# Float32r parts for the weights-times-values products of an attention kernel, and three shared buffers for weight chunks and their low parts

## The chip, the cores and the metric

The kernel runs on one core of a Trainium2 chip. The metric is the device time of one execution in microseconds (us). A core has TensorE (PE, which also has a queue of weight loads, PEld), VectorE (DVE), ScalarE (ACT), GpSimd (POOL) and SyncE (SP, which here only issues DMAs). Each engine works through its own instructions in the order of its queue.

## The reference

Two blocks of two layers each run after one another on 512 tokens of 1024 features, in float32. What the change touches is the last step of every softmax attention: weights times values.

```python
# block 1, a layer: window attention and latent attention, 8 heads each, 512 tokens and 256 context tokens
p = jax.nn.softmax(jnp.concatenate([s_loc, s_ctx, s_sink], axis=-1), axis=-1)
o = (jnp.einsum('bnhgqk,bnkhd->bnqhgd', p_loc, vw) + jnp.einsum('bnhgql,blhd->bnqhgd', p_ctx, v_ctx))
...
p = jax.nn.softmax(s.astype(jnp.float32) * SCALE_B, axis=-1)
return jnp.einsum('bhqk,bkhd->bqhd', p.astype(vals.dtype), vals)
# block 2, a layer: two softmax mixers (6 heads each), a gated recurrence, then a gated feed-forward
return jnp.einsum('bhgqk,bhkd->bhgqd', p, vt)
...
return (jax.nn.silu(a) * b) @ w_down
```

All projections (in_proj, the branches' merge, w_o, w_up, w_down) are plain matrix products with weights from DRAM.

## The kernel before

Features lie on partitions, tokens along the free dimension. A projection `h @ w` is worked off in chunks of weights of 128 x 1024 values (512 KB). `wload` (L149 and on) fetches one: a DMA brings it into a buffer `wraw` (issued on SP, L162), ACT casts it to a float32r high part `wh` (`hi`, L139), and DVE subtracts that from the chunk, in two halves of 512 columns, to give the float32r low part `wl` (`lo`, L144). `mm3` (L174 and on, the product in L182) then multiplies by three of the four pairs of parts (high x high, high x low, low x high): 24 matmuls for each chunk and 512 tokens. `self.wb = (2, 2)` (in `block1`) gives two buffers to `wraw`, and two each to `wh` and `wl`. Chunks that are kept for later lie in tiles of another tag; of these only `wraw` comes from these buffers.

Block 1's first layer has 768 columns (tokens and context), its second layer 512. A layer goes through `attention` (scores, softmax, `pv_out`, with projections filled in between), `merge` (for each of 3 branches and 8 feature tiles a gate projection of one chunk, and a branch product of half a chunk: a branch chunk serves two feature tiles, so it is in use over half a product, a whole gate product and half a product), and `w_out`. Block 2's layers go through `mixers`, a `w_out_2` product in two halves of the tokens, and `ffn` (44 chunks of w_up, then 24 of w_down, of which every third is 384 KB). While `merge` and the first layer's `ffn` run, a generator `mod_steps` computes modulation vectors on DVE (L294) from further 512 KB loads (`mw`, L289).

`pv_out` (L527 and on) takes the normalised weights of two query tiles j = 0, 1 of one head. It transposes them on TensorE, 128 x 128 at a time and four to a group, into a PSUM tile `pt` (2 buffers), copies the group to SBUF in one ACT instruction (`pT`, 3 buffers), and multiplies each transposed tile by the values of its key block, in float32: values of 64 columns as the stationary operand, the two query tiles in the two halves of the array's columns, so of `pv`'s partitions. In the trace a float32 product is two matmul instructions. Two DVE copies (L547) take `pv` to `y`.

`schedule_with_timeline_sim=True`: the order of each queue, and which buffer of a tag a tile gets, are fixed when the kernel is built. SP's queue holds all loads and stores of the kernel, in one order.

Of the kernel before, what the change touches and what calls it, by code (L numbers as in the profile page):

```python
# [9 lines left out]
F32 = mybir.dt.float32  # L10
# [6 lines left out]
P = 128  # L17
# [13 lines left out]
class Cat:  # L31
    """Column ranges of one feature tile kept in two tiles, split at column 512."""
# [10 lines left out]
class Pools:  # L43
    """Two pools as one: the tags named lie in the second."""
# [8 lines left out]
class Halves:  # L53
    """A chunk of weights in two tiles of 512 columns."""
# [13 lines left out]
class Fill:  # L68
    """Steps of generators, emitted a few at a time among the steps of another stream."""
# [34 lines left out]
class Kern:  # L104
# [10 lines left out]
    def open(self):  # L115
# [5 lines left out]
        self.ones = self.cp.tile([P, P], F32, tag="ones", name="ones")  # L121
# [27 lines left out]
    def wload(self, src, kt, n, tag=None):  # L149
        """A chunk [128, kt*n] of weights as an exact sum of two float32r parts."""  # L150
# [23 lines left out]
    def mm3(self, ps, w, x, cols, n0=0, n1=P, ks=None, start=True, stop=True, o=0):  # L174
        """ps[n, t - o] += sum_k w[k][:, n] x[k][:, t] from split operands."""
# [9 lines left out]
    def seq(self, a, b):  # L185
        """Keeps b behind a in their engine's queue."""
# [3 lines left out]
    def after(self, ins):  # L190
        """Keeps ins behind the last product so far."""
# [3 lines left out]
    def rsqrt(self, v, n, inv, pool=True):  # L195
        """(v*inv + eps)^-0.5 of a small [128, n]: a first guess from the exponent, one step of third order, one of second."""
# [9 lines left out]
        # y * (15 - 10 a + 3 a^2) / 8  # L206
# [20 lines left out]
    def colsum(self, ps, a, nt):  # L227
        """ps[p, t] = sum over the partitions of a[:, t*128 + p]."""
# [3 lines left out]
    def rows(self, ps, r, nt):  # L232
        """ps[m, t*128 + p] = r[p, t] for every m."""
# [5 lines left out]
    def silu_cols(self, src, n, name, w):  # L239
        """[128, 8, w] with silu of n vectors in the first n columns, zeros elsewhere."""  # L240
        nc = self.nc
        c = self.kp.tile([P, KD, n], F32, tag=src, name=src)
        nc.sync.dma_start(c, self.A[src])
        t = self.kp.tile([P, KD, n], F32, tag=name + "_t", name=name + "_t")
        nc.scalar.activation(t, c, AF.Tanh, scale=0.5)
        s = self.kp.tile([P, KD, w], F32, tag=name, name=name)
        if w > n:
            nc.vector.memset(s, 0.0)
        u = self.kp.tile([P, KD, n], F32, tag=name + "_u", name=name + "_u")
# [4 lines left out]
    def mod_chunk(self, sc, n, wsrc, bias, layer, g, mt):  # L254
        """mt[:, 8g:8g+8, :] = 1024 outputs of s @ w + b for n vectors, on the tensor engine."""
# [10 lines left out]
        self.mod_rows(ps, n, bias, g, mt)  # L266

    def mod_rows(self, ps, n, bias, g, mt):
        """Output 256j + c of vector r, in row 32j + r and column c of ps, to features on partitions, plus bias."""
        nc = self.nc  # L270
        row = self.sm.tile([P, 256], F32, tag="modrow", name=self.nm("modrow"), bufs=1)
# [4 lines left out]
        # feature g*1024 + j*256 + s*128 + p sits in column s*128 + j*32 + r  # L276
# [6 lines left out]
    def mod_steps(self, sc, n, wsrc, bias, layer, g, mt):  # L283
        """The same with the products on the vector engine; one step a 128 rows of w."""
# [16 lines left out]
        self.mod_rows(ps, n, bias, g, mt)  # L301
# [37 lines left out]
    def norm_part(self, xs, mod, g, c0, c1, j, ishift, iscale, dst, tmp=None, acc=None, sq="t"):  # L339
        """Columns c0:c1 of h = rms_norm(x, g) * (1 + scale) + shift, split into the tiles that dst(k) gives; mod  # L340
# [1526 lines left out]
```

## Time and profile before

| | us |
|---|---|
| median of 3 runs | 3027.91 (3026.98 to 3037.3) |
| span of the profiled execution | 3026.6 |
| TensorE busy in it | 2920.6 |
| VectorE busy | 1924.7 |
| ScalarE busy | 1353.0 |

The profiled execution's span lies 1.3 us under the median of the runs; what lies around the span is within that, so a change of the span is taken as a change of the time. In the profile's rows a busy PE is not PE at its peak, since matmuls overlap: the spacing of their starts tells what one costs. The letters f32 and fp32r in a row's shapes are the operands' types; matmuls of float32r operands are printed as f32 too.

### The profile page before, as it was taken

To read this page: it belongs to the slowest core of one execution; us is meant where nothing else is said; L and a number is where in the kernel's file an instruction comes from. 1 tells how busy PE (TensorE), PEld (TensorE's weight loads), DVE (VectorE), ACT (ScalarE), POOL (GpSimd) and SP (SyncE) were. 2 spreads that over 40 slices of the span, in tenths; PEclk is the share of its full clock that TensorE was granted. 3 is DMA by queue.
4 is the path that set the end of the run, shared out by engine and by line. 5 is a ranking of instruction groups with operands and counts; after the bars stand their busy time and mean duration, and the time that the engine had idled before them with its cause. 6 is when DMAs were issued, how large, how long until landed. Compare 5 with 4: busy or idle time off the path is not lost.

```text
span 3026.6 us, 46233 instructions
## 1 busy us (share of the span) xinstructions
PE 2920.6 (96%) x17920; PEld 2417.4 (80%) x17920; DVE 1924.7 (64%) x3720; ACT 1353.0 (45%) x2414; POOL 261.5 (9%) x520
## 2 busy tenths in 40 slices
PE   7999999999998999999998998999999998999999
PEld 4888888888887888777778876788888876788887
DVE  5666555555556566656676777688853778576642
ACT  3445544322234345653225775544433675554421
POOL 2000000001112000000112212000000223000000
PEclk9999999999998999999999999999999999999999
DMA  6221111333342423124653211355543311233232
GB/s 236 76 69 53 55 63 64 116 127 124 119 160 85 126 80 106 52 69 174 232 201 132 76 47 48 105 177 200 189 142 115 97 43 53 85 100 97 98 107 89
DMA packets 113163, 331.76 MB, mean 110 GB/s; under 512 B 18160, under 2 KB 20720, under 8 KB 112944
## 3 DMA queue, kind: packets, MB, share of 16 engines
q1 hardware_dynamic: 112944, 328.81, 33.6%
q8 instruction: 141, 2.31, 0.3%
q14 instruction: 78, 0.64, 0.1%
HBM read 300.51 MB, written 17.76 MB: 105 GB/s over the span
## 4 chain that ended last, share of the span: by engine, by line
PE 84%; DVE 8%; ACT 2%; DMA 2%; issue 2%; POOL 2%; SPq 0%; DVEq 0%; ACTq 0%; POOLq 0%
PE mm L182 32%; PE up L182 15%; PE dn L182 11%; PE pu L182 5%; PE pv L544 4%; PE pt L539 4%; PE po L182 2%; PE s L851 2%; PE s L568 1%; PE s L1223 1%; DVE zz L1527 1%; DVE wl L144 1%; PE pre L182 1%; PE pq L182 1%; DMA yg<-yd 1%
## 5 line engine op out<-in xcount | busy, mean ns | idle before, releaser
L144 DVE TENSOR_TENSOR wl<-wraw,wh 128x512 fp32r<-128x512 f32 (+2 forms) x706 | 473.1, 709 | 391.3 <-ACT wh L139 382.8
L139 ACT CAST wh<-wraw 128x1024 fp32r<-128x1024 f32 (+4 forms) x364 | 365.8, 1005 | 754.2 <-PE mm L182 241.5
L182 PE MATMUL mm<-hh,wh 128*128 128x512 f32 (+1 forms) x1240 | 488.8, 397 | 9.2 <-ACT hh L373 3.5
L182 PE MATMUL mm<-hl,wh 128*128 128x512 f32 (+1 forms) x1240 | 487.9, 394 | 5.0 <-DVE hl L374 5.0
L182 PE MATMUL mm<-hh,wl 128*128 128x512 f32 (+1 forms) x1240 | 487.3, 393 | 0.0
L182 PEld LDWEIGHTS mm<-hh,wh 128*128 128x128 f32 x1240 | 235.0, 191 | 58.2 <-ACT wh L139 6.9
L182 PEld LDWEIGHTS mm<-hl,wh 128*128 128x128 f32 x1240 | 235.8, 190 | 50.3 <-DVE hl L374 7.0
L182 PEld LDWEIGHTS mm<-hh,wl 128*128 128x128 f32 x1240 | 235.5, 190 | 49.6 <-DVE wl L144 3.0
L182 PE MATMUL up<-hh,wh 128*128 128x512 f32 (+1 forms) x688 | 261.1, 381 | 3.8 <-DVE fu L1643 2.3
L182 PE MATMUL up<-hl,wh 128*128 128x512 f32 (+1 forms) x688 | 261.0, 380 | 0.5
L182 PE MATMUL up<-hh,wl 128*128 128x512 f32 (+1 forms) x688 | 261.2, 380 | 0.2 <-DVE wl L144 0.2
L541 ACT COPY pT<-pt 128x512 f32<-128x512 f32 (+1 forms) x304 | 159.5, 551 | 177.0 <-PE pt L539 175.7
L294 DVE SCALAR_TENSOR_TENSOR macc<-mw,sc,macc 128x1024 f32<-128x1024 f32 x140 | 181.0, 1308 | 74.1 <-DMA mw<-w_mod 38.8
L539 PE MATMUL pt<-ident,E 128*128 128x128 f32 x1120 | 174.7, 282 | 4.1 <-DVE E L551 3.4
L539 PEld LDWEIGHTS pt<-ident,E 128*128 128x128 f32 x1120 | 127.8, 142 | 39.6 <-issue 24.4
L182 PEld LDWEIGHTS up<-hh,wh 128*128 128x128 f32 x688 | 128.8, 188 | 30.2 <-ACT ah L139 2.7
L182 PEld LDWEIGHTS up<-hl,wh 128*128 128x128 f32 x688 | 129.1, 188 | 26.2 <-DVE hl L374 1.3
L182 PEld LDWEIGHTS up<-hh,wl 128*128 128x128 f32 x688 | 129.1, 188 | 25.8 <-DVE wl L144 0.9
L964 POOL TENSOR_TENSOR m<-m,gt 128x768 f32<-128x768 f32 (+1 forms) x32 | 54.5, 1704 | 1077.4 <-DVE gt L960 755.8
L182 PE MATMUL mm<-ch,wl 128*128 128x256 f32 x504 | 143.7, 285 | 0.0
L182 PE MATMUL mm<-cl,wh 128*128 128x256 f32 x504 | 143.2, 284 | 0.0
L182 PE MATMUL mm<-ch,wh 128*128 128x256 f32 x504 | 143.1, 284 | 0.0
(416 smaller groups left out, 6135.7 us busy)
## 6 DMA issues: line engine op xcount, KB each, us to landing
wraw<-w_in SPq DMA_DIRECT2D x158, 512.0 KB, 3.5
mw<-w_ada SPq DMA_DIRECT2D x96, 512.0 KB, 4.4
wraw<-w_up SPq DMA_DIRECT2D x88, 512.0 KB, 3.5
mw<-w_mod SPq DMA_DIRECT2D x32, 512.0 KB, 3.5
wraw<-w_down SPq DMA_DIRECT2D x32, 512.0 KB, 3.5
wraw<-w_branch SPq DMA_DIRECT2D x24, 512.0 KB, 3.7
wraw<-w_out SPq DMA_DIRECT2D x22, 512.0 KB, 3.5
wraw<-w_o SPq DMA_DIRECT2D x19, 512.0 KB, 3.7
```

The costliest lines, as they stand in the source:

```text
L139: self.nc.scalar.copy(out, in_)
L144: (eng or self.nc.vector).tensor_tensor(out, in_, hi.bitcast(F32), op=ALU.subtract)
L182: self.last = self.nc.tensor.matmul(ps[: n1 - n0, c0 - o:c1 - o], lhsT=a[:, k, n0:n1], rhs=b[j][:, c0:c1], start=start and i == 0, stop=st ...
L294: nc.vector.scalar_tensor_tensor(acc[r], w, sc[:, k, r:r + 1], acc[r], op0=ALU.mult, op1=ALU.add)
L539: nc.tensor.transpose(pt[:, o * P:o * P + P], ecol(j, kb), self.ident)
L541: nc.scalar.copy(tt[:, :n], pt[:, :n])
L544: nc.tensor.matmul(pv[64 * j:64 * j + 64, :P], lhsT=vst(kb), rhs=tt[:, o * P:o * P + P], start=i == ends[j][0], stop=i == ends[j][-1])
L568: nc.tensor.matmul(s[:, c0:c1], lhsT=q[:, i * P:(i + 1) * P], rhs=kp[:, a0:a0 + c1 - c0], start=pi == 0, stop=pi == 1)
L851: self.nc.tensor.matmul(ps, lhsT=a[:96, i * P:(i + 1) * P], rhs=b[:96, c0:c1], start=pi == 0, stop=pi == 2)
L964: nc.gpsimd.tensor_tensor(ms[n][:, :tn], ms[n][:, :tn], m[:, :tn], op=ALU.add)
L1223: nc.tensor.matmul(s, lhsT=q[:, i * P:(i + 1) * P], rhs=kp, start=pi == 0, stop=pi == 1)
L1527: self.nc.vector.tensor_tensor(z[rows, h].rearrange("p (b u x) -> p b u x", u=2, x=H), q[rows].rearrange("p (b u x) -> p b u x", u=2, x=H) ...
```

## The change

- `wload`: the DMA's buffer is taken from the tag `wl`, with 3 buffers (`self.wb = (3, 2)`), and the low part's tile from the same tag, after the DMA. `wh` keeps its 2. So 5 buffers stand where 6 stood.
- Values are kept as float32r high and low parts side by side, 64 + 64 columns (`vpair`, `vsplit`): ACT writes the high parts, DVE the low ones.
- `pv_out`: a transposed group leaves PSUM twice, as a float32r high part (ACT, `hi`) and a float32r low part (DVE, `lo`), with 4 buffers for both. For each key block and each of these parts one matmul multiplies the value parts (128 columns) with the columns of both query tiles (256). High and low values' results lie in the two halves of `pv`'s partitions; ACT copies the one to `y`, and DVE adds the other. Key blocks that only one query tile needs come last.
- Besides, `modrow` lies in a buffer of `mw` (or of another tag), `ones` has one column, the two masks become one, the vectors of `silu_cols` move to another pool. In the window attention the last query tile's context scores lie ahead of the local ones, so that one mask serves.

```diff
-                h, l = (self.wp.tile([P, 1024], F32R, tag=t, name=self.nm(t), bufs=self.wb[1]) for t in ("wh", "wl"))
-        raw = self.wp.tile([P, 1024], F32, tag="wraw", name=self.nm("wraw"), bufs=self.wb[0])
+                h, l = self.wp.tile([P, 1024], F32R, tag="wh", name=self.nm("wh"), bufs=self.wb[1]), None
+
+        raw = self.wp.tile([P, 1024], F32, tag="wl", name=self.nm("wraw"), bufs=self.wb[0])
         nc.sync.dma_start(raw[:, :c], src)
+        l = l or self.wp.tile([P, 1024], F32R, tag="wl", name=self.nm("wl"), bufs=self.wb[0])
...
-        self.va = self.bp.tile([P, 6, 2, 64], F32, tag="v", name=self.nm("va"), bufs=3)
+        self.va = self.vpair("va")
...
+    def vpair(self, name):
+        return self.bp.tile([P, 6, 2, 2, 64], F32R, tag="v", name=self.nm(name), bufs=3)
+
+    def vsplit(self, v, src):
+        self.hi(v[:, :, :, 0], src)
+        self.lo(v[:, :, :, 1], src, v[:, :, :, 0])
...
     def pv_out(self, blocks, ecol, vst, y, row, q0):
         pv = self.ps.tile([P, 512], F32, tag="pv", name=self.nm("pv"), bufs=1)
+        blocks = [b for b in blocks if len(b[1]) == 2] + [b for b in blocks if len(b[1]) == 1]
...
-            tt = self.ptp.tile([P, 512], F32, tag="pT", name=self.nm("pT"), bufs=3)
-            nc.scalar.copy(tt[:, :n], pt[:, :n])
-            for o, (kb, j) in enumerate(grp):
-                i = g + o
-                nc.tensor.matmul(pv[64 * j:64 * j + 64, :P], lhsT=vst(kb), rhs=tt[:, o * P:o * P + P],
-                                 start=i == ends[j][0], stop=i == ends[j][-1])
-        for j in range(2):
-            nc.vector.tensor_copy(y[row:row + 64, q0 + P * j:q0 + P * j + P], pv[64 * j:64 * j + 64, :P])
+            th, tl = (self.ptp.tile([P, 512], F32R, tag="pT", name=self.nm("pT" + x), bufs=4) for x in "hl")
+            self.hi(th[:, :n], pt[:, :n])
+            self.lo(tl[:, :n], pt[:, :n], th[:, :n])
+            at = [o for o, (kb, j) in enumerate(grp) if not o or grp[o - 1][0] != kb]
+            for u, t in enumerate((th, tl)):
+                for o in at:
+                    kb, j = grp[o]
+                    m = P * sum(k == kb for k, _ in grp)
+                    nc.tensor.matmul(pv[:, P * j:P * j + m], lhsT=vst(kb), rhs=t[:, o * P:o * P + m],
+                                     start=g == o == u == 0, stop=g + 4 >= len(todo) and u == 1 and o == at[-1])
+        out = y[row:row + 64, q0:q0 + 256]
+        nc.scalar.copy(out, pv[64:128, :256])
+        nc.vector.tensor_tensor(out, pv[0:64, :256], out, op=ALU.add)
...
-        vs = [self.bp.tile([P, 6, 2, 64], F32, tag="v", name=self.nm("vb"), bufs=3) for _ in range(2)]
+        vs = [self.vpair("vb") for _ in range(2)]
...
-                nc.scalar.copy(vs[g][:, t], src[:, g])
+                self.vsplit(vs[g][:, t:t + 1], src[:, g:g + 1])
...
-        self.wb = (2, 2)
+        self.wb = (3, 2)
...
-        self.mod_rows(ps, n, bias, g, mt)
+        self.mod_rows(ps, n, bias, g, mt, self.bp.tile([P, 1024], F32, tag="mw", name=self.nm("modrow"), bufs=self.bb["mw"]))
```

## Rows read from the trace of the kernel before

**Rows 1.** The page, part 2: TensorE's busy share in 40 slices of 75.7 us.
```profile
PE   7999999999998999999998998999999998999999
```

**Rows 2.** Busy time by stretches (stretch: length, PE, PEld, DVE, ACT, POOL, PEclk, DMA share, GB/s).
```profile
1400.00:1570.00 170.00, 168.86 (x762) 134.01 (x761) 118.04 (x149) 48.55 (x63) 18.83 (x13) 1.00 0.67 229
...
1700.00:1775.00 75.00, 70.75 (x600) 52.64 (x599) 64.31 (x158) 51.39 (x101) 23.76 (x43) 0.98 0.17 50
...
1850.00:1920.00 70.00, 61.87 (x471) 45.19 (x470) 48.17 (x120) 39.93 (x83) 15.96 (x36) 0.95 0.18 53
...
2060.00:2210.00 150.00, 150.00 (x685) 121.75 (x684) 128.63 (x189) 61.60 (x81) 0.00 (x0) 1.00 0.58 202
...
2660.00:2880.00 220.00, 219.20 (x1074) 185.57 (x1073) 150.34 (x240) 94.23 (x132) 2.16 (x11) 1.00 0.30 95
```

**Rows 3.** Waits of SP's queue, 2660 to 2880 us (in total, times, longest).
```profile
SPq L162 <- DVE wl L144: 199.4, 37, 17.5
```

**Rows 4.** Timelines of ACT, DVE, SP, second feed-forward (start, duration, instruction, idle before).
```profile
2747.26 1.05 ACT L139 CAST wh<-wraw 128x1024 fp32r<-128x1024 f32 x1 [3.57 <-issue]
...
2758.14 1.05 ACT L139 CAST wh<-wraw 128x1024 fp32r<-128x1024 f32 x1 [3.57 <-issue]
...
2748.35 1.29 DVE L144 TENSOR_TENSOR wl<-wraw,wh 128x512 fp32r<-128x512 f32 x2 [2.56 <-ACT wh L139]
...
2749.71 0.33 SPq L162 DMA_DIRECT2D wraw<-w_up  x1
```

**Rows 5.** DMA issues (us to landing): 2660-2880, 1960-2210, 1400-1570, whole page.
```profile
wraw<-w_up SPq DMA_DIRECT2D x39, 512.0 KB, 3.4
...
wraw<-w_up SPq DMA_DIRECT2D x42, 512.0 KB, 3.7
...
wraw<-w_branch SPq DMA_DIRECT2D x10, 512.0 KB, 4.4
...
wraw<-w_down SPq DMA_DIRECT2D x16, 384.0 KB, 3.1
```

**Rows 6.** Timelines of ACT and DVE in the first feed-forward.
```profile
2109.15 1.06 ACT L139 CAST wh<-wraw 128x1024 fp32r<-128x1024 f32 x1 [3.40 <-PE up L182]
...
2111.17 1.28 DVE L144 TENSOR_TENSOR wl<-wraw,wh 128x512 fp32r<-128x512 f32 x2
```

**Rows 7.** Timeline of ACT in the first w_out_2 product; one cast between these two.
```profile
1932.41 1.05 ACT L139 CAST wh<-wraw 128x1024 fp32r<-128x1024 f32 x1 [2.65 <-PE dn L182]
...
1938.33 1.05 ACT L139 CAST wh<-wraw 128x1024 fp32r<-128x1024 f32 x1 [1.17 <-PE dn L182]
```

**Rows 8.** Timeline of PE in the first layer's latent attention.
```profile
307.87 0.28 PE L182 MATMUL pk<-kvh,wl 128*128 128x256 f32 x1
307.99 0.28 PE L182 MATMUL pk<-kvh,wh 128*128 128x256 f32 x1
...
313.16 0.39 PE L182 MATMUL mm<-hh,wl 128*128 128x512 f32 x1
313.39 0.39 PE L182 MATMUL mm<-hh,wh 128*128 128x512 f32 x1
313.71 0.66 PE L544 MATMUL pv<-pT,va 128*64 128x128 f32 x8
314.30 0.50 PE L182 MATMUL mm<-hl,wh 128*128 128x512 f32 x1
```

**Rows 9.** Groups of instructions by line and form (count, busy us, mean ns, idle before).
```profile
L544 PE MATMUL pv<-pT,va 128*64 128x128 f32 x1408 | 114.4, 285 | 6.6 <-DVE y L547 3.6 <-ACT pT L541 2.8
...
L544 PE MATMUL pv<-pT,vb 128*64 128x128 f32 x832 | 63.8, 283 | 0.3 <-ACT pT L541 0.2
...
L541 ACT COPY pT<-pt 128x512 f32<-128x512 f32 x272 | 151.2, 585 | 147.9 <-PE pt L539 146.7 <-ACT pT L541 0.2
...
L547 DVE COPY y<-pv 64x128 f32<-64x128 f32 x256 | 73.6, 288 | 71.7 <-PE pv L544 68.1
...
L960 DVE SCALAR_TENSOR_TENSOR gt<-gt,pu 128x512 f32<-128x512 f32 x32 | 21.8, 681 | 3.5 <-PE pu L182 3.5
```

More of the change, by code (lines that the diff above doesn't have):

```diff
@@ L120, in open @@
         self.ident = self.const("ident", [P, P])
-        self.ones = self.cp.tile([P, P], F32, tag="ones", name="ones")
+        self.ones = self.cp.tile([P, 1], F32, tag="ones", name="ones")
         nc.vector.memset(self.ones, 1.0)
@@ L265, in mod_chunk, with mod_rows @@
                                      start=k == 0, stop=k == KD - 1)
-        self.mod_rows(ps, n, bias, g, mt)
-    def mod_rows(self, ps, n, bias, g, mt):
+        self.mod_rows(ps, n, bias, g, mt, self.hblk(F32, "modrow") if g == 0 else self.blk("E", name="modrow"))
+    def mod_rows(self, ps, n, bias, g, mt, row):
         nc = self.nc
-        row = self.sm.tile([P, 256], F32, tag="modrow", name=self.nm("modrow"), bufs=1)
+        row = row[:, :256]
         nc.vector.tensor_copy(row, ps[:, :256])
@@ L507, in a_kv @@
                 nc.tensor.transpose(pt[:, (t - t0) * P:(t - t0 + 1) * P], vf[:, t * P:(t + 1) * P], self.ident)
-            nc.scalar.copy(self.va[:, t0:t1], pt[:, :(t1 - t0) * P].rearrange("p (t h d) -> p t h d", t=t1 - t0, h=2))
+            src = pt[:, :(t1 - t0) * P].rearrange("p (t h d) -> p t h d", t=t1 - t0, h=2)
+            self.vsplit(self.va[:, t0:t1], src)
+    def vpair(self, name):
[3 more added lines that the diff above has]
+        self.lo(v[:, :, :, 1], src, v[:, :, :, 0])
     def a_q(self, p, tn, ps=None):
@@ L531, in pv_out @@
         pv = self.ps.tile([P, 512], F32, tag="pv", name=self.nm("pv"), bufs=1)
+        blocks = [b for b in blocks if len(b[1]) == 2] + [b for b in blocks if len(b[1]) == 1]
         todo = [(kb, j) for kb, js in blocks for j in js]
-        ends = [[i for i, (_, j) in enumerate(todo) if j == q] for q in range(2)]
         for g in range(0, len(todo), 4):
@@ L565, in a_pair @@
             s = self.pss.tile([P, 1024], F32, tag="s", name=self.nm("s"), bufs=1)
-            for c0, c1, a0 in ((512 - nl, 512, k0 * P), (512, 768, 512)):
+            for c0, c1, a0 in ((512 - nl, 512, k0 * P), (512, 768, 512)) if i < 3 else ((256, 512, 512), (512, 768, k0 * P)):
                 for pi, kp in enumerate(self.ka[kv]):
@@ L570, in a_pair @@
             e = self.blk("E")
-            mask = self.maskb if i == 3 else self.maska[:, 640 - w:]
+            mask = self.mask[:, :w] if i == 3 else self.mask[:, 896 - w:]
             nc.vector.tensor_tensor_reduce(e[:, :w], s[:, 512 - nl:768], mask, op0=ALU.add, op1=ALU.max, scale=1.0,
@@ L585, in ecol @@
             e, w, nl = es[j]
-            c = (kb - spans[j][0]) * P if kb < 4 else nl + (kb - 4) * P
+            own, other = (0, nl) if i0 + j < 3 else (CTX, 0)
+            c = own + (kb - spans[j][0]) * P if kb < 4 else other + (kb - 4) * P
             return e[:, c:c + P]
@@ L653, in attention @@
             self.a_kv()
[L654 removed]
+        self.mask = self.const("mask", [P, 896])
         F.add(self.latents(tn))
@@ L1198, in head_rows, with values @@
         return ps
-    def values(self, ps, nh, name, tag="pt"):
+    def values(self, ps, nh, name, tag="pt", parts=False):
         nc = self.nc
@@ L1204, in values @@
         nc.scalar.copy(f, ps)
-        v = self.bp.tile([P, 4, nh, 64], F32, tag=name, name=self.nm(name), bufs=2)
         pt = self.ps1("vt", tag)
@@ L1208, in values @@
             nc.tensor.transpose(pt[:, t * P:(t + 1) * P], f[:, t * P:(t + 1) * P], self.ident)
-        nc.scalar.copy(v, pt.rearrange("p (t h d) -> p t h d", t=4, h=nh))
+        src = pt.rearrange("p (t h d) -> p t h d", t=4, h=nh)
+        if parts:
+            v = self.bp.tile([P, 4, nh, 2, 64], F32R, tag=name, name=self.nm(name), bufs=2)
+            self.vsplit(v, src)
+            return v
+        v = self.bp.tile([P, 4, nh, 64], F32, tag=name, name=self.nm(name), bufs=2)
+        nc.scalar.copy(v, src)
         return v
@@ L1228, in attn2_unit @@
         self.pv_out([(kb, [0, 1]) for kb in range(4)], lambda j, kb: es[j][:, kb * P:(kb + 1) * P],
-                    lambda kb: v[:, kb, kv, :], y, row, i0 * P)
+                    lambda kb: v[:, kb, kv].rearrange("p u d -> p (u d)"), y, row, i0 * P)
     def mix_done(self, i, y):
@@ L1309, in a_prep @@
                 yield 5.1
-                self.va = self.values(self.proj2(4), 2, "va2", "s")
+                self.va = self.values(self.proj2(4), 2, "va2", "s", True)
             else:
@@ L1365, in c_vals @@
     def c_vals(self):
-        self.cva = self.values(self.proj2(19), 2, "va2")
+        self.cva = self.values(self.proj2(19), 2, "va2", parts=True)
         yield 5.1
```

27 lines of the change are left out of this document (12 added, 15 removed).

## The prediction

> **What bounds the kernel now.** I read the page's slices first: TensorE is busy nine tenths or more nearly everywhere [rows 1]. The table by stretches then says where something else is near: in the merge of the second layer and in both feed-forwards PE has no gap, DVE is at 69%, 86% and 68% of its time; only at the start of block 2's mixers is DVE at 64.3 of 75 us [rows 2]. So PE's own work sets the time, and two things can move it: how much work there is, and whether operands are there. For the second I read SP's waits and a timeline. A weight load waits for DVE's low part, 199 us in total in the second feed-forward [rows 3], but harmlessly: a low part starts at 2748.35 and takes 1.29, the load that waits for it goes out at 2749.71, 0.07 later, takes 3.4 us [rows 4, 5], and is there at 2753.1; its cast only comes at 2758.14 [rows 4], when PE frees `wh`. That is 5 us of reserve, less than one chunk of PE time: two chunks take 10.88 us from cast to cast, 5.44 each [rows 4].
>
> **The products.** 2240 instructions on L544 are busy for 178 us [rows 9]; they are 1120 products, since two make one. By groups: from 313.39 to 314.30 are 0.91 us, less 0.23 for the matmul of 512 columns ahead (its spacing), 0.68 for four products [rows 8]; 272 full groups [rows 9] make 185, and the 32 single products of the window attention (8 heads, 2 units, 2 layers) 0.36 each, 12 more: 197 (one product's two instructions, and the same rest). Inside a group the spacing is only (0.66 - 0.28) / 7 = 0.054 [rows 8] (0.28 is the mean duration of one [rows 9]), 121 us in all; the rest is change-over at the group's ends. After: 544 pairs of products take two matmuls of 256 columns each at 0.12 [rows 8], 131 us; the 32 single ones two matmuls of 128 columns, which no row shows: between a quarter of 0.23 and all of it, 4 to 15. Together 135 to 146. The gain is 178 - 140 = 38 us; it lies between 62 (197 - 135, change-over gone) and -25 (121 - 146, change-over stays).
> The Trainium skill, "TensorEngine Tiling (Array Packing)", section "When to Use Tiling", speaks against giving up column tiles: a stationary operand of 64 columns should be packed two to the array, for up to twice the rate. The spacing of 0.054 agrees that the old form had that [rows 8]; by this rule alone the change gains nothing, the bound of -25.
>
> **Getting the weights out of PSUM.** ACT's copy of a group becomes a cast of the same size (0.585 [rows 9]); DVE gets a subtraction for each of 304 groups, 0.68 by the DVE instruction of 512 columns that reads PSUM [rows 9], and loses 256 copies of 0.288 [rows 9] for 128 additions of 256 columns, between 0.288 and 0.68, say 0.43. With the values' low parts (4 of 0.68, 48 at most 0.3, six smaller) DVE gets 199 - 74 + 55 + 20 = 200 us, 10% more; ACT some 50. A group's `pt` is held 0.8 us longer, and a product waits behind whatever DVE has queued. In block 1 DVE has room. At the start of the mixers about 7 units add 1.2 each, 9 us, to 64.3 of 75 [rows 2]: full. The cost lies between 0 and 30 us (two such stretches and the second latent attention); I take 10.
>
> **The three buffers.** While PE works on chunk n, its low part holds one, the landed chunk n+1 a second, and that chunk's low part needs the third. Load n+2 can only go out when low part n+1 is made (its raw buffer frees) or chunk n is finished: one whole chunk later than now. SP's queue is one, so modulation loads and stores behind it are late too. A chunk's chain is load 3.4 + 0.07 + cast 1.05 + 0.04 + low part 1.29 + 0.07 = 5.92 [rows 4, 5] (the 0.07 after landing is taken from the other handover), and none of it overlaps with the next if a load always waits for the low part ahead. If it may wait for the end of chunk n, two chains overlap and PE needs the first half only: (5.44 + 0.07 + 5.28) / 2 = 5.40 a chunk. Which buffer a load gets is fixed when the kernel is built, and the trace of before can't show it; so each stage has two ends:
> - Second feed-forward: 5.40 against 5.44, nothing; or 0.48 for some 35 chunks after the reserve is used up, 17.
> - First feed-forward: loads take 3.7 [rows 5], and between cast and low part lie up to 0.96 us (2110.21 to 2111.17 [rows 6]), since DVE is at 86%. (5.51 + 3.7 + 0.07 + 1.05 + 0.5 + 0.65 + 0.07) / 2 = 5.78, so 0.34 for 38 chunks, 13; or 7.14 a chunk, 65.
> - w_down, 16 tiles of 24 + 24 + 18 matmuls of 0.23 [rows 8] = 15.2: chains of 5.92, 5.92 and 5.2 (load 3.1 [rows 5], the rest by 768 columns) are 17.0, 27 in all; or 2.
> - Merge of the second layer: a branch chunk holds its buffer over 2.7 + 5.44 + 2.7. Stepped through from the end of a gate product at 0: the next gate's low part ends at 2.4, the branch load goes out, takes 4.4 [rows 5], and its product starts at 8.8. The load after it goes out at 8.3 (the gate product's end) or 9.4 (the low part); 4.4 + 1.1 + 0.8 later, at 14.6 or 15.7, PE goes on, which ended that product at 11.5: 3.1 to 4.2 idle, and 0.4 before. Eleven such rounds: 39 to 50, with DVE's queue up to 60.
> - First layer's merge, 8.2 + 4.1 a round: 0 to 10; projections ahead of its second layer: 0 to 6.
> - w_out_2, chunks of 256 columns, 2.8 of PE: now one each 2.96 (5.92 / 2 [rows 7]), already a bound of the loads. After, (2.8 + 0.07 + 5.28) / 2 = 4.1, or 5.9: 1.1 for 9 chunks, twice, 20; or 50.
> Sum 74 to 235. I take 145: loads before long stretches will mostly wait for low parts, but DVE's queue is shorter where PE waits.
>
> **The sum.** 3026.6 - 38 + 10 + 145 = 3143.6 for the span, 1.3 more for the median: 3145 us.
>
> **Rivals.**
> 1. The other side: the loads stay hidden and the products' gain is all that is seen. Mechanism: the chain of a chunk fits into PE's 5.44 because loads wait for chunk ends and land sooner; it decides at a load of 2.9 us or less in the always-waiting form, and no row shows 512 KB under 3.4 [rows 5]. Time: 3027.9 - 38 = 2990, with the full change-over 2966. Against it stands the merge, which idles in either form. 0.12.
> 2. They cancel: low ends in every stage (74) against a gain of 62 and no cost on DVE: 3040, within 15 us. 0.08.
> 3. Evacuation binds instead: products wait for DVE in all attention, loads near their low end. 304 groups exposed by a third of their 0.68 cost 69: 3027.9 + 74 - 38 + 69 = 3133, at another place. 0.07.
> 4. The products get no cheaper (25 dearer instead of 38 cheaper): 3145 + 63 = 3208. 0.05.
> 5. The clock falls in the new gaps. Where PE was busy 61.9 of 70 us the granted clock was 0.95 on the mean [rows 2], a tenth of the stretch at 1.2 GHz instead of 2.4; that costs half a tenth, 3.5 us of 70. Over some 430 us of merge, first feed-forward and w_out_2: 21, so 3166. 0.10. The Trainium skill, "TensorE: Matmul & The Clock Gate", section "HAM oscillation — how this bites in real kernels", says that waits for loads between bursts of matmuls bring the low clock back for each burst; rows 2 agree that it falls where PE has gaps.
>
> **How the numbers follow.** The forecast has 0.58; rivals 3, 4 and 5 (0.22) are slower too. Slower by over 0.5%, which is about what a measurement of this kernel can tell from no change, has 0.80, the same 0.08, faster 0.12. The range leaves out rival 1 and the ends' ends: from 3027.9 + 74 - 62 = 3040 to 3027.9 + 235 + 25 + 30 = 3318, of which the sum of all worst ends is unlikely; 3045 to 3245.
>
> **What would show it.** The waits of SP on L162 in the second feed-forward should name DVE (or PE), and PE's gaps in that stage `wh` or `wl`, from none now [rows 2]; two chunks take over 11.5 us if loads wait for low parts, 10.9 if not. The merge of the second layer should show a gap of 3 to 4 us in each round. L544 should take some 140 us with spacing 0.12, and the starts around it should lose their change-over. The mixers should show DVE full. Wrong is the prediction if casts in the feed-forwards start right after PE frees `wh`, as now: then the loads are still hidden, and the time lies under 3020.

## The result and the profile after

The changed kernel takes 3231.12 us (median; 3222.58 to 3233.97) against 3028.86 us for the kernel before on the same chip: a ratio of 1.066, with a 95% interval of 1.0644 to 1.0675. The forecast was 3145, inside a range of 3045 to 3245. The profiled execution spans 3232.1 us, 205.5 more than before, and TensorE's mean granted clock is 0.966 of full speed where it was 0.986.

The chain that ended last changed its make-up. The page, part 4, of the kernel before, and under it that of the changed kernel (shares of the span by engine):

```profile
PE 84%; DVE 8%; ACT 2%; DMA 2%; issue 2%; POOL 2%; SPq 0%; DVEq 0%; ACTq 0%; POOLq 0%
```

```profile
PE 58%; DMA 16%; DVE 12%; ACT 8%; issue 3%; POOL 1%; SPq 1%; ACTq 0%; DVEq 0%; POOLq 0%
```

TensorE lost 26 points, to transfers (+14), ScalarE (+6) and VectorE (+4): a chunk's load, cast and low part now stand on the path. The line numbers below are those of each kernel: the load is L162 before and L163 after, and lines further down move by up to 24.

**One chunk in the second feed-forward.** Timelines of ScalarE, VectorE and SP in the changed kernel (start, duration, instruction, idle before), which answer to [rows 4]:

```profile
2932.50 1.05 ACT L139 CAST wh<-wraw 128x1024 fp32r<-128x1024 f32 x1 [3.78 <-DMA wraw<-w_up]
2938.50 1.05 ACT L139 CAST wh<-wraw 128x1024 fp32r<-128x1024 f32 x1 [1.69 <-DMA wraw<-w_up]
...
2933.59 1.29 DVE L144 TENSOR_TENSOR wl<-wraw,wh 128x512 fp32r<-128x512 f32 x2 [2.81 <-ACT wh L139]
...
2934.95 6.32 SPq L163 DMA_DIRECT2D wraw<-w_up  x2
```

The low part ends at 2934.88; the next load goes out at 2934.95; the cast that it feeds starts at 2938.50, 6.00 us after the one ahead of it. In the kernel before two chunks took 10.88 us [rows 4]. The waits say the same. Waits of SP's queue, 2830 to 3080 us of the changed kernel (in total, times, longest), which answer to [rows 3]:

```profile
SPq L163 <- DVE wl L144: 213.8, 37, 8.9
```

That line alone is no proof, since before it read 199.4 and cost nothing [rows 3]. What is new is who waits behind the load. Waits of ScalarE in the same stretch of the changed kernel:

```profile
ACT wh L139 <- DMA wraw<-w_up: 92.1, 36, 4.1
```

In the kernel before, from 2660 to 2880 us, no cast into `wh` waited for a load: it waited 57.2 us for what the profile calls issue and 6.5 us for TensorE to free the buffer.

**The stages.** I divided the span by the first and last products into `pu` (merge), `po` (w_o), `dn` and `up`, as the timelines show them. Five of these stretches, first of the kernel before, then of the changed one (columns as in [rows 2]): merge of the second layer, its w_o, the first mixers, the first and the second feed-forward.

```profile
1398.00:1582.00 184.00, 182.82 (x821) 144.86 (x820) 129.97 (x163) 52.01 (x69) 20.61 (x15) 1.00 0.68 232
1582.00:1637.00 55.00, 53.14 (x424) 50.85 (x422) 33.56 (x66) 31.51 (x68) 8.34 (x17) 1.00 0.46 149
...
1681.00:1899.00 218.00, 203.49 (x1614) 152.84 (x1612) 165.75 (x385) 145.78 (x266) 59.43 (x103) 0.97 0.18 53
...
1962.00:2214.00 252.00, 248.46 (x1234) 205.81 (x1234) 216.18 (x331) 107.51 (x150) 2.16 (x11) 1.00 0.56 190
...
2655.00:2899.00 244.00, 242.59 (x1184) 204.74 (x1183) 168.85 (x273) 105.68 (x150) 2.16 (x11) 1.00 0.30 97
```

```profile
1412.00:1622.00 210.00, 192.40 (x821) 150.32 (x822) 125.59 (x164) 55.16 (x70) 21.30 (x15) 0.96 0.59 205
1622.00:1697.00 75.00, 62.02 (x421) 58.05 (x420) 29.53 (x57) 28.52 (x60) 7.14 (x16) 0.89 0.29 91
...
1746.00:1974.00 228.00, 204.06 (x1443) 158.24 (x1442) 189.07 (x410) 153.89 (x285) 53.01 (x103) 0.96 0.18 55
...
2058.00:2330.00 272.00, 262.30 (x1234) 208.37 (x1233) 219.35 (x329) 109.48 (x151) 3.12 (x11) 0.97 0.53 176
...
2819.00:3088.00 269.00, 261.37 (x1184) 202.57 (x1184) 168.46 (x270) 109.20 (x152) 3.05 (x11) 0.99 0.28 86
```

Read the count beside PE's busy time, not the busy time alone. In the second feed-forward 1184 matmuls took 242.59 us before and "261.37 us" after: the busy time grew with the stretch. A matmul of 512 columns is shown 0.39 us long and the next one starts 0.23 after it, so a start that is late by up to 0.16 leaves no gap; and 86 of the 1184 are shown as longer than 0.4, where before none was. By busy share that stage went from 99% to 97%; by matmuls a microsecond from 4.85 to 4.40.

All stages, in us, with the experiments that are told below:

| stage | before | changed | e1 | e2 | e3 | e4 |
|---|---|---|---|---|---|---|
| first layer up to its merge | 585 | 583 | 593 | 574 | 570 | 585 |
| merge | 294 | 296 | 294 | 295 | 294 | 295 |
| w_o | 74 | 79 | 77 | 75 | 75 | 74 |
| second layer up to its merge | 445 | 454 | 457 | 449 | 437 | 439 |
| merge | 184 | 210 | 209 | 207 | 198 | 186 |
| w_o | 55 | 75 | 72 | 72 | 61 | 60 |
| start of block 2 | 44 | 49 | 49 | 50 | 47 | 46 |
| first mixers | 218 | 228 | 219 | 230 | 224 | 215 |
| w_out_2 | 63 | 84 | 75 | 82 | 73 | 67 |
| feed-forward, up | 252 | 272 | 270 | 265 | 251 | 252 |
| w_down | 125 | 141 | 142 | 134 | 125 | 125 |
| second mixers | 252 | 263 | 264 | 261 | 260 | 249 |
| w_out_2 | 64 | 85 | 79 | 77 | 77 | 66 |
| feed-forward, up | 244 | 269 | 274 | 250 | 246 | 247 |
| w_down | 124 | 140 | 143 | 135 | 123 | 123 |

A step of a few us between two neighbours can be the border's, where the end of one stage runs beside the start of the next. Each column is one execution, and the order of the queues is fixed anew for each kernel; that too can move a stage by some us.

**The new work.** Groups of the changed kernel (count, busy us, mean ns, idle before), which answer to [rows 9] (here `<-PE pv` in the second line is new: the cast waits until a product gives back a buffer of `pT`):

```profile
L144 DVE TENSOR_TENSOR pTl<-pt,pTh 128x512 fp32r<-128x512 f32 (+1 forms) x304 | 194.2, 643 | 50.7 <-ACT pTh L139 49.0
L139 ACT CAST pTh<-pt 128x512 fp32r<-128x512 f32 (+1 forms) x304 | 164.8, 551 | 134.4 <-PE pt L551 91.9 <-PE pv L560 35.2 <-DVE sm L1422 2.3
L564 DVE TENSOR_TENSOR y<-pv,y 64x256 f32<-64x256 f32 x128 | 53.0, 414 | 32.2 <-ACT y L563 30.3
L563 ACT COPY y<-pv 64x256 f32<-64x256 f32 x128 | 47.1, 368 | 77.8 <-PE pv L560 75.5
```

### The profile page after: what moved, and what is told of

Read it like the earlier page. It is cut to its first block, busy times and chain, and to the rows that moved or that the text cites. A ratio compares the mean times of both kernels' runs of the same rounds, so it can differ in the third digit from the quotient of the medians.

```text
span 3232.1 us, 44279 instructions
## 1 busy us (share of the span) xinstructions
PE 2995.7 (93%) x16832; PEld 2475.9 (77%) x16832; DVE 2071.0 (64%) x3952; ACT 1419.0 (44%) x2542; POOL 253.9 (8%) x520
## 4 chain that ended last, share of the span: by engine, by line
PE 58%; DMA 16%; DVE 12%; ACT 8%; issue 3%; POOL 1%; SPq 1%; ACTq 0%; DVEq 0%; POOLq 0%
PE mm L184 25%; PE up L184 9%; DMA wraw<-w_down 5%; PE pu L184 5%; DVE wl L144 4%; ACT wh L139 4%; DMA wraw<-w_up 4%; PE dn L184 3%; PE pv L560 3%; DMA wraw<-w_in 3%; PE pt L551 3%; PE po L184 2%; PE s L870 2%; DVE pTl L144 1%; PE s L586 1%
## 5 line engine op out<-in xcount | busy, mean ns | idle before, releaser
L184 PE MATMUL up<-hh,wh 128*128 128x512 f32 (+1 forms) x688 | 269.4, 394 | 11.7 <-ACT wh L139 10.1
L184 PE MATMUL up<-hh,wl 128*128 128x512 f32 (+1 forms) x688 | 270.1, 393 | 2.8 <-DVE wl L144 2.7
L144 DVE TENSOR_TENSOR pTl<-pt,pTh 128x512 fp32r<-128x512 f32 (+1 forms) x304 | 194.2, 643 | 50.7 <-ACT pTh L139 49.0
L139 ACT CAST pTh<-pt 128x512 fp32r<-128x512 f32 (+1 forms) x304 | 164.8, 551 | 134.4 <-PE pt L551 91.9
L551 PE MATMUL pt<-ident,E 128*128 128x128 f32 x1120 | 182.3, 282 | 17.0 <-DVE pTl L144 7.8
L551 PEld LDWEIGHTS pt<-ident,E 128*128 128x128 f32 x1120 | 135.0, 145 | 29.5 <-DVE pTl L144 8.7
L184 PE MATMUL dn<-ah,wh 128*128 128x512 f32 (+1 forms) x358 | 142.4, 398 | 15.0 <-ACT wh L139 14.9
```

The costliest lines, as they stand in the source:

```text
L139: self.nc.scalar.copy(out, in_)
L144: (eng or self.nc.vector).tensor_tensor(out, in_, hi.bitcast(F32), op=ALU.subtract)
L184: self.last = self.nc.tensor.matmul(ps[: n1 - n0, c0 - o:c1 - o], lhsT=a[:, k, n0:n1], rhs=b[j][:, c0:c1], start=start and i == 0, stop=st ...
L551: nc.tensor.transpose(pt[:, o * P:o * P + P], ecol(j, kb), self.ident)
```

## The experiments

Theory: nearly all the loss is the shared buffers, by the serial chain of load, cast and low part; products and evacuation together change little. Rival: the evacuation in two parts costs much of it. Each kernel is compared with the kernel before on the same chip (3030.2 to 3031.2 us).

**e1: the buffers alone, in the kernel before.**

```diff
-h, l = (self.wp.tile([P, 1024], F32R, tag=t, name=self.nm(t), bufs=self.wb[1]) for t in ("wh", "wl"))
-raw = self.wp.tile([P, 1024], F32, tag="wraw", name=self.nm("wraw"), bufs=self.wb[0])
+h, l = self.wp.tile([P, 1024], F32R, tag="wh", name=self.nm("wh"), bufs=self.wb[1]), None
+raw = self.wp.tile([P, 1024], F32, tag="wl", name=self.nm("wraw"), bufs=self.wb[0])
 nc.sync.dma_start(raw[:, :c], src)
+l = l or self.wp.tile([P, 1024], F32R, tag="wl", name=self.nm("wl"), bufs=self.wb[0])
...
-self.wb = (2, 2)
+self.wb = (3, 2)
```

> The kernel before with one part of the change alone: a chunk of weights and its low part come from one set of three buffers; transposes, products and values are as before. Theory (the shared buffers are the whole loss, because a load waits until the low part of the chunk before it is made, and load, cast and low part run one behind the other): 3195 to 3240 us, the feed-forward of the second layer at 6.0 us a chunk. By the prediction's own term (145) it would be 3174. Rival (the loss of the changed kernel lies in the evacuation of the weights in two parts, and the buffers cost a half or less of it): 3060 to 3130 us.

Measured: 3217.98 us, ratio 1.0609 (1.0589 to 1.0629), that is 187 us of the 202. Waits of ScalarE in its second feed-forward, 2830 to 3070 us:

```profile
ACT wh L139 <- DMA wraw<-w_up: 97.0, 36, 5.2
```

The same wait, as long as in the changed kernel. The rival is out as the main cause. All the rest of the change, its smaller moves included, adds about 15 us beside this (1.066 against 1.0609; the intervals lie 0.0015 apart).

**e2: the changed kernel with the cast in two halves.**

```diff
-for a in range(0, c, 512 if halves else 1024):
-    e = min(c, a + (512 if halves else 1024))
+for a in range(0, c, 512):
+    e = min(c, a + 512)
     self.hi(h[:, a:e], raw[:, a:e])
```

> The changed kernel with ScalarE's cast of a chunk of weights made in two halves of 512 columns, so that the low part's first half starts when the first half is cast; nothing else differs, and the load still waits for the whole low part. Theory (the serial chain load, cast, low part sets the pace wherever weights are streamed): the chain falls from the 6.03 us measured in the second layer's feed-forward to about 3.4 + 0.07 + 0.6 + 0.04 + 1.3 + 0.07 = 5.5, against 5.44 that TensorE needs; the loss of 202 us falls to a third or less, 3060 to 3110 us. Rival (the time is lost to the evacuation, or to transfers that are themselves slower): 3200 us or more, since ScalarE has more instructions.

Measured: 3167.63 us, ratio 1.045 (1.0429 to 1.0472). A third of the loss is gone where two thirds or more were expected: the direction bears the theory out, the size does not. Timelines of ScalarE and VectorE of this kernel, second feed-forward:

```profile
2883.59 1.14 ACT L139 CAST wh<-wraw 128x512 fp32r<-128x512 f32 x2 [0.32 <-DMA wraw<-w_up]
...
2889.34 1.15 ACT L139 CAST wh<-wraw 128x512 fp32r<-128x512 f32 x2 [3.93 <-DMA wraw<-w_up]
...
2884.24 1.29 DVE L144 TENSOR_TENSOR wl<-wraw,wh 128x512 fp32r<-128x512 f32 x2 [0.25 <-ACT wh L139]
```

The chain is now 5.75 us here, not 5.5: the low part starts 0.65 after the cast, and a load takes 3.6 (median of this stage), not 3.4. In this stage most of the loss is gone all the same (269 to 250 us; 244 before). In the first feed-forward 13 of 20 us stay: modulation loads stand on SP between the loads of weights there, and VectorE has other work between cast and low part; no run separates the two. The merge stays as it was (207): by the prediction's steps its branch chunk holds a buffer over two more chunks' time, which a shorter cast does not change. So the serial chain counts, but only the plain stream is set by its sum alone.

**e3: the changed kernel with six half buffers.** The same memory, cut finer:

```diff
-raw = self.wp.tile([P, 1024], F32, tag="wl", name=self.nm("wraw"), bufs=self.wb[0])
-nc.sync.dma_start(raw[:, :c], src)
-l = l or self.wp.tile([P, 1024], F32R, tag="wl", name=self.nm("wl"), bufs=self.wb[0])
+rt = [self.wp.tile([P, S], F32, tag="wl", name=self.nm("wraw"), bufs=self.wb[0]) for _ in range(0, c, S)]
+raw = Halves(rt, n)
+for i, t in enumerate(rt):
+    nc.sync.dma_start(t[:, :min(S, c - S * i)], src[:, S * i:min(c, S * i + S)])
+low = l is None
+l = Halves([self.wp.tile([P, S], F32R, tag="wl", name=self.nm("wl"), bufs=self.wb[0]) for _ in range(0, c, S)], n) if low else l
...
-self.wb = (3, 2)
+self.wb = (6, 2)
```

Cast and low part are made half by half as well.

> The changed kernel with the same 12 KB a partition cut into six shared buffers of 512 columns in place of three of 1024: a chunk comes as two loads, each cast and subtracted by itself, so that the first load of the next chunk goes out when the first half of the low part is done. Theory: the chain of a half (load under 3.4, cast 0.6, low part 0.65) is 4.5 us or less against 5.44, so TensorE is the bound again where weights are streamed, and the time falls to 3015 to 3050 us; the faster products show only if this comes out under the kernel before with the same halves. Rival (twice the DMAs and more instructions on ScalarE cost as much as they free): 3100 us or more.

**e4: the kernel before with the same half buffers.** The diff is that of e3 on the older lines, with `self.wb` from (2, 2) to (6, 2).

> The kernel before with six shared buffers of 512 columns (12 KB a partition beside 8 KB of high parts, where it had 16 KB beside 8), and nothing else of the change. Theory: the supply is no bound, within 1% of the kernel before (3010 to 3060 us). Against the changed kernel with the same buffers it prices the products and their evacuation: by the prediction's terms (-38 and +10) the changed one is 28 us faster; by what its attention stages showed (no gain) the two lie within 20 us. Rival: the halves cost 60 us or more in either kernel.

Measured: e3 3073.3 us, 1.0135 (1.012 to 1.0151); e4 3034.93 us, 1.0013 (1.0004 to 1.0022). Waits of ScalarE in e3's second feed-forward, 2700 to 2930 us:

```profile
ACT wh L139 <- PE up L185: 70.2, 21, 3.7
...
ACT wh L139 <- DMA wraw<-w_up: 1.6, 3, 1.2
```

The casts wait for TensorE again, as they should, and feed-forwards and w_down are back at their old lengths (table). With 4 KB a partition less than before, e4 is within 0.22% of the kernel before: it was the size of the pieces that cost the time, not the bytes. e3 lies between the ranges of its theory and its rival. What was not expected is its distance from e4: with no supply in the way, the rest of the change (products, evacuation and the smaller moves) makes the kernel 38 us slower, where the prediction had products and evacuation 28 us faster. By stages e3 gains 15 us on e4 in the first layer and loses 9 and 11 in the mixers and 6 and 11 in the w_out_2 behind them; in the second layer of block 1 it loses 12 in the merge and gains 2 ahead of it. That merge holds no product of this kind, and it is about as long in the kernels below that have no subtraction (e5, 199 us) or the new products in the first layer alone (e10, 195), against 186 in e4. So some 10 us there hardly belong to the products or their evacuation. The smaller moves of the change, such as `modrow` in a buffer of `mw`, stand in all of these kernels and not in e4; no run takes them out, so their part stays open.

**e5: e3 without the subtraction.**

```diff
-th, tl = (self.ptp.tile([P, 512], F32R, tag="pT", name=self.nm("pT" + x), bufs=4) for x in "hl")
+th = tl = self.ptp.tile([P, 512], F32R, tag="pT", name=self.nm("pTh"), bufs=4)
 self.hi(th[:, :n], pt[:, :n])
-self.lo(tl[:, :n], pt[:, :n], th[:, :n])
```

> The changed kernel with half buffers (3073 us), without VectorE's subtraction that makes the low part of the attention weights: both products of a group take the high part, so the low part of the weights is left out of the result while TensorE issues as many products as before. It prices the evacuation by itself. In the parent the products hold TensorE 194 us from start to start, of which 1152 at 0.12 us are 138, against 171 us in the kernel before with the same buffers. Theory (the products are cheaper, but they wait for the subtraction, and in the mixers VectorE is full with it): the 56 us of waits go for the most part, 3005 to 3035 us. Rival (the cost lies in the products' form, in the clock or in the two-step evacuation of the output): 3055 us or more.

**e9: e5 with the subtraction made and not read.**

```diff
 th, tl = (self.ptp.tile([P, 512], F32R, tag="pT", name=self.nm("pT" + x), bufs=4) for x in "hl")
+lost, tl = tl, th
 self.hi(th[:, :n], pt[:, :n])
-self.lo(tl[:, :n], pt[:, :n], th[:, :n])
+self.lo(lost[:, :n], pt[:, :n], th[:, :n])
```

> As the run without the subtraction (both products of a group take the high part of the weights, so their low part is left out of the result; 3021 us), but VectorE still makes the low part, which nothing reads: its 304 subtractions stand in VectorE's queue and hold the transposes' PSUM buffers, and no product waits for them. Theory 1 (their load on VectorE, and what comes later behind them there, is the 52 us): 3060 us or more. Theory 2 (the products' wait for a second step behind ScalarE's copy is the cost): 3021 to 3035 us. Between the two, the shares can be read from the time.

Measured: e5 3020.91 us, 0.9968 (0.9958 to 0.9978); e9 3056.09 us, 1.0083 (1.0064 to 1.0103). e9 lies between its two ranges, next to the first. So the subtraction costs 3073 - 3021 = 52 us: 35 of them (3056 - 3021) while nothing waits for its result, by its load on VectorE and the time that it holds the transposes' PSUM buffer, and 17 (3073 - 3056) once the products read it. The intervals leave some 6 us of doubt in either share. The 17 hold more than the products' own wait: a group takes two of four `pT` buffers where it took one of three, and in e3 14 casts wait 25.3 us until a product gives one back; in e9 and e5 none does (0.4 us in e4). What more `pT` buffers would give back, no run shows. The stretches of the two mixers, of e3, e9, e5 and e4 in this order (DVE is the third busy time, after PE and PEld):

```profile
1682.00:1906.00 224.00, 202.72 (x1437) 158.10 (x1437) 189.47 (x408) 154.60 (x299) 55.26 (x103) 0.95 0.19 55
2355.00:2615.00 260.00, 233.00 (x1616) 182.66 (x1616) 212.11 (x456) 175.88 (x337) 58.90 (x121) 0.97 0.21 63
```

```profile
1689.00:1913.00 224.00, 203.60 (x1456) 158.53 (x1455) 188.07 (x408) 155.56 (x302) 55.26 (x103) 0.96 0.18 56
2357.00:2613.00 256.00, 232.65 (x1638) 184.19 (x1637) 210.33 (x456) 175.46 (x339) 60.40 (x122) 0.97 0.20 64
```

```profile
1667.00:1881.00 214.00, 199.46 (x1445) 156.92 (x1444) 172.74 (x374) 158.81 (x309) 56.30 (x103) 0.96 0.17 54
2324.00:2576.00 252.00, 230.51 (x1623) 181.05 (x1623) 188.72 (x420) 177.70 (x343) 58.77 (x122) 0.97 0.20 63
```

```profile
1685.00:1900.00 215.00, 201.03 (x1610) 151.68 (x1609) 167.39 (x385) 146.96 (x280) 57.62 (x103) 0.98 0.19 58
2344.00:2593.00 249.00, 234.55 (x1796) 180.19 (x1794) 190.53 (x435) 168.76 (x320) 61.05 (x122) 0.97 0.22 66
```

With the subtraction, read or not, the two mixers take 480 to 484 us; without it 466, about the length of the old form (464). VectorE is busy some 20 us more in each with it, 85 and 82% of the stretch. That mean hides where it is out of time. Forty us near the start of each of the mixers in e3, then of the first ones in e4, and later in the first ones of e5:

```profile
1722.00:1762.00 40.00, 34.62 (x304) 26.29 (x303) 39.67 (x94) 27.83 (x59) 14.06 (x28) 1.00 0.13 41
2429.00:2469.00 40.00, 36.54 (x319) 27.99 (x318) 39.67 (x95) 27.98 (x59) 14.43 (x30) 0.96 0.13 41
```

```profile
1725.00:1765.00 40.00, 35.70 (x351) 26.68 (x350) 39.25 (x95) 27.87 (x59) 16.53 (x31) 1.00 0.14 41
```

```profile
1823.00:1863.00 40.00, 34.67 (x352) 27.23 (x351) 39.17 (x76) 24.81 (x53) 18.77 (x32) 0.87 0.09 30
```

VectorE is full there with the subtraction (39.67 of 40), but nearly so in the old form too (39.25), and in e5 somewhat later (39.17). So its share alone does not tell what lengthens a stage; the waits say more. Waits of TensorE in e3 from 1682 to 1979 us:

```profile
PE s L1248 <- DVE sm L1419: 4.2, 4, 2.5
PE s L1248 <- DVE sm L1357: 3.8, 3, 1.5
PE pv L561 <- DVE pTl L144: 3.8, 4, 1.8
PE pv L561 <- DVE y L565: 3.3, 3, 2.5
```

Only the third line is a product that waits for its weights' low part; the fourth is the output's addition, which holds the one `pv` buffer. The first two are the softmax of later units. They are not the subtraction's doing: in the same stages of e5, which has none, TensorE waits 9.1 us for `sm` there, against 8.0. What the subtraction does add is seen in the waits of TensorE over the whole of e9, and under them of e5:

```profile
PE pv L562 <- ACT pTh L139: 11.2, 19, 1.9
PE pt L552 <- DVE pTl L144: 10.3, 8, 1.8
```

```profile
PE pv L560 <- ACT pTh L139: 3.0, 10, 0.4
```

The transposes wait for a PSUM buffer that the subtraction still reads, and products wait longer for the cast. That is 18 us of the 35 at most, since in e5 the transposes wait longer for the softmax's `E` (6.4 us, 1.8 in e9); where the rest lies the waits don't say.

**e6: e3 with the normalising on ScalarE**, and **e7: e3 with transposes ahead of products.** Two attempts to take back what e3 loses, one on each half of the cause.

```diff
-self.nc.vector.tensor_scalar(e, e, r, None, op0=ALU.mult)
+self.nc.scalar.activation(e, e, AF.Copy, scale=r)
```

```diff
 for g in range(0, len(todo), 4):
-    product(*turn(g))
+    t = turn(g)
+    if due:
+        product(*due)
+    due = t
+product(*due)
```

Here `turn` stands for the lines with the transposes, the cast and the subtraction of a group, `product` for those with its matmuls.

> The changed kernel with half buffers (3073 us), with the 304 or so products of a row of weights with its factor (the normalising, 0.50 us each on VectorE, some 22 us of VectorE in each layer's mixers) moved to ScalarE; nothing else. Theory 1 (VectorE's load is what the evacuation costs): 3040 to 3060 us. Theory 2 (it is the latency of copy and subtraction between a group's transposes and its products, whatever else VectorE does): within 10 us of 3073, or slower, since ScalarE also makes the copies for which TensorE waits.

> The changed kernel with half buffers (3073 us), where the transposes of a unit's next group of four stand ahead of the products of the group before in TensorE's order; the work is the same. Theory 2 (the latency of copy and subtraction, some 1.3 us, stands between transposes and products): the next group's 0.44 us of transposes and its own work cover a part of it in every unit of two or three groups, 3045 to 3062 us. Theory 1 (VectorE is full in the mixers): 3065 us or more, since VectorE has as much to do.

Measured: e6 3068.93 us, 1.0131 (1.0114 to 1.0149), no difference from e3 that the intervals tell; e7 3074.23 us, 1.0143 (1.0128 to 1.0158), the same. (The normalising is 256 instructions, not 304.) The two mixers of e6:

```profile
1679.00:1908.00 229.00, 205.57 (x1440) 159.10 (x1439) 173.71 (x370) 178.66 (x340) 50.28 (x103) 0.94 0.18 54
2360.00:2618.00 258.00, 229.71 (x1619) 179.85 (x1617) 195.60 (x416) 198.60 (x377) 55.02 (x122) 0.98 0.20 64
```

VectorE got 16 us of its time back in each mixer and the stage did not get shorter, 229 and 258 us: ScalarE, which makes the casts of the attention weights and of the chunks, took over 23 to 24 (155 to 179, 176 to 199). By its time e6 lies in the range of theory 2 and e7 in that of theory 1, so neither theory holds by itself: here less work on VectorE was worth nothing, since the next engine in the same chain got it. e7 moved waits within the chain and did not shorten them: from the first mixers to the end of the w_out_2 behind them a product waits 2.8 us for `pTl` there (3.8 in e3), and the tile `s` for the softmax 10.7 (8.0). Whether an engine off the chain could take the work at a gain was not tried.

**e8: e3 with the old products in block 2 alone**, and **e10: the new products in the first layer of block 1 alone.** Both are e3 with the older `pv_out`, values and single copy where the new ones are left out (`two` is set in the first layer alone):

```diff
-self.pv_out([(kb, [0, 1]) for kb in range(4)], lambda j, kb: es[j][:, kb * P:(kb + 1) * P],
-            lambda kb: v[:, kb, kv].rearrange("p u d -> p (u d)"), y, row, i0 * P)
+self.pv_old([(kb, [0, 1]) for kb in range(4)], lambda j, kb: es[j][:, kb * P:(kb + 1) * P],
+            lambda kb: v[:, kb, kv, :], y, row, i0 * P)
```

```diff
 def pv_out(self, blocks, ecol, vst, y, row, q0):
+    if not self.two:
+        return self.pv_old(blocks, ecol, vst, y, row, q0)
```

> The changed kernel with half buffers (3073 us), where the mixers of the second block make their products as the kernel before did (float32 weights from one copy, 64-column products), and the first block as the changed one. Theory (the change gains in the first block, where VectorE is busy 69% of the time, and loses in the mixers, where it is busy 85%): the mixers and what follows them give back 9 + 6 + 11 + 11 us, 3025 to 3045 us, near the kernel before. Rival (the loss is spread over all attention): 3050 to 3070 us.

> The kernel before with half buffers (3035 us), with the new products and weights in two parts in the first layer of the first block alone, where the changed kernel's stage was 15 us shorter (585 to 570 us up to the first merge) and VectorE was busy 69% of the time; the second layer of that block and all mixers make their products as before. Theory (the change pays where VectorE has time): 3017 to 3025 us, under both kernels. Rival (that stage's gain came from elsewhere, or is given back in the merge behind it): 3030 us or more.

Measured: e8 3035.72 us, 1.0013 (1.0001 to 1.0024); e10 3023.23 us, 0.9973 (0.9962 to 0.9984). Both lie in the theory's ranges. Giving block 2 its old products back is worth 38 us; keeping the new ones only in the first layer, where VectorE is busy 69% of the time (393.33 of 570 us in e3), gives 12 us on e4. e10 is under both kernels, by 0.27% and 6.4%, in the 20 KB a partition of weight buffers that the changed kernel has; its first layer is 572 us long where e4's is 585. The two runs show in which layers the new form pays. That VectorE's free time is the reason fits, but no run changes that alone.

## Why the prediction came out as it did

**The sum.** The sign, the main cause and the range held; the middle was 86 us low, and the time lies 14 us under the range's upper end. The terms: buffers +145, measured +187; products -38 and evacuation +10, together -28, where all the rest of the change measured about +15 beside the buffers' stalls and +38 without them. The two parts do not add: 187 + 38 = 225 against 202. VectorE may catch up in time that is lost to loads; no run shows it.

**Which end of the chain.** The prediction left open whether a load may go out at a chunk's end or must always wait for the low part. The trace settles it for the second feed-forward: 37 of its loads wait for the low part, with 0.07 us between, as worked out. In the first one 33 do, and 6 wait for TensorE. The chain of 5.92 was measured as 6.00 between those two casts, with a load of 3.47 (2934.95 to 2938.42, when the waiting queues are released).

**The stages of the buffers**, e1 less before, against the two ends: second feed-forward 30 (0 to 17), first 18 (13 to 65), w_down 36 in all (2 to 27), merge of the second layer 25 (39 to 60), first merge 0 (0 to 10), w_out_2 27 in all (20 to 50), the stages ahead of the two merges 20 (0 to 6 for the second), and 38 in stages that had no term: the second layer's w_o 17, the first one's 3, the start of block 2 5, the mixers 1 and 12. Together 194, of 195 between the spans of the two profiled executions. Four steps failed.
- Second feed-forward: 0.48 for 35 chunks. In the changed kernel it is 0.56 for all 44, 25 us; no reserve covers the first ones, and a load took 3.6 in its median, not 3.4.
- w_down: 17.0 us a tile was too little (and 16 times 1.8 are 29, not 27). 142 - 125 and 143 - 124 for eight tiles each are 2.1 and 2.4 a tile more than before, not 1.8 at most. In the changed kernel loads of 512 KB took 3.7 and 3.8 here, not 3.4; they also stand on SP among the stores of the tiles before, whose part is not separated.
- Merge: the steps had a branch load of 4.4 [rows 5]. It took 3.8 in the changed kernel, and the gate's load 3.3, where transfers are less dense (DMA share 0.59 where it was 0.68). The stage grew by 26 us, not by 3 to 4 in each of eleven rounds. By the same steps with these two times eleven rounds would be 27 to 33, an estimate: the loads' times, read from a stage that did not stall, were most of the miss.
- Forgotten: w_o streams its chunks through the same buffers. The sum asked of the stages that it named, not of every caller of the load.

**The products.** The spacing is 0.12 us for 256 columns, as taken; 1088 of them and 64 of half the size at that pace would be 134 us. From the start of each to the start of TensorE's next instruction they hold it 194 us in e3, against 171 for the older 2240 in e4: the step that failed is not the matmul's price but the view that the group's ends vanish. Without the subtraction (e5) it is still 169, of which TensorE stands still 5.9 us for the output's addition and 3.0 for the cast. Most of the rest lies where TensorE goes over to another tile: 212 such places hold 46 us, 0.22 each where the spacing is 0.12. So with the subtraction left out the two forms differ by 14 us in the whole kernel (3035 and 3021), in favour of the new one, not by 38. The Trainium skill, "TensorEngine Tiling (Array Packing)", section "When to Use Tiling", gives a stationary operand of 64 columns two column tiles, as the old form had them. No loss shows from giving them up: the 14 us are a gain, and the new form fills the columns with the values' two parts instead.

**The evacuation.** This is the term that was mis-sized: 10, with 30 as its end, measured 52. The prediction counted VectorE's time and asked where it exceeds 100%: one stretch of 75 us at the start of the mixers [rows 2]. VectorE did fill up there, but the loss is not only there. By stages (e3 less e5) 18 us lie in the mixers, 14 in the two w_out_2, and some 13 in block 1 ahead of its two merges (one execution of each kernel). The sum named the PSUM buffer that is held longer but put a price on it in two or three stretches only, and it did not ask whether four `pT` buffers are enough for two to a group. A third of each subtraction exposed, as rival 3 put it (69 us), was nearer. Against it e9 shows that two thirds of the cost are there although no product waits for the subtraction's result.

**The clock.** Rival 5 gave 21 us. The granted clock did fall where TensorE has long gaps: 0.89 in the second layer's w_o, busy 62.02 of 75 us, from 1.00; 0.94 in the second mixers, from 0.97. In the feed-forwards, which lose time in every chunk, it fell only from 1.00 to 0.97 and 0.99. The Trainium skill, "TensorE: Matmul & The Clock Gate", section "HAM oscillation — how this bites in real kernels", tells of a kernel that waits longer for its loads than it computes between them, and meets the low clock after each wait. The second feed-forward, at 0.56 us lost in 6.00, is not of that kind. By rival 5's own working, one less the granted clock times the stretch, the whole kernel gives 110 us after (0.034 of 3232.1) against 42 before (0.014 of 3026.6). The 68 us between are an estimate from above, since part of the low clock falls on gaps. So the clock can be up to a third of the loss, more than the 21 us that rival 5 took for a few stages. No run separates it; the 187 us contain it.

**What would show it.** SP's wait names VectorE, a chunk takes 6.00 us (over 11.5 for two), the spacing is 0.12: as written. Wrong were the gaps of the merge (smaller) and the 140 us of the products (194). VectorE was full at the start of the mixers, as written, but not in all of them.

## To carry to other kernels

When buffers are merged, write down for each which event frees it and follow the loop once round: a chain of load, cast and low part that just exceeds the consumer's time costs its excess in every chunk, in every stage that goes through the same routine. Before giving up such a saving, cut the pieces finer: six half buffers in the room of three whole ones gave back all that the feed-forwards and w_down had lost. Price an added operation by the chain it enters and by the buffers that it holds, and read its engine's share in short stretches: a mean of 85% held 40 us at 99%.

## What the runs showed that was not expected

- TensorE's busy time hides a lack of operands: 1184 matmuls "took" 242.59 us in the kernel before and 261.37 in the changed one, with the same work, since matmuls are shown longer than the distance of their starts; the count a microsecond shows the loss, the share does not.
- Two loads of 256 KB in place of one of 512 KB cost nothing measurable beyond e4's 0.13%: in e3's first feed-forward 85 halves land in 3.1 us each (median), where a whole takes 3.6 to 3.7, and both are under way together.
